# Attention's first two groups stored unsplit through GpSimd's queue, and split later

## The chip, the cores and the metric

The kernel runs on one NeuronCore of a Trainium2 chip. Its engines work side by side, each through its own queue of instructions in order: TensorE (PE in the profile; its weight loads are PEld), VectorE (DVE), ScalarE (ACT), GpSimd (POOL) and SyncE (SP), which here only issues DMAs. Time is device time of one execution in microseconds. The kernel before took 1574.63 us in the median of three runs (1574.16 to 1576.02).

## The reference, cut to what matters

One decoder block in float32, for 1024 tokens of width 1024:

```
h = rms_norm(x);  proj = h @ w_in + b_in     # ret q,k,v,gate | attn q,k,v | gate_a, gate_b
branch_a = (silu(rg) * group_norm(retention(rotary(rq), rotary(rk), rv))) @ w_ret_out
aq, ak = rotary(aq), rotary(ak)              # 16 query heads, 2 key/value heads, 64 wide
ay = softmax_with_sink(band128(aq @ ak^T / 8)) @ av
branch_b = ay.reshape(S, 1024) @ w_attn_out
x = x + (sigmoid(gate_a)*branch_a + sigmoid(gate_b)*branch_b) @ w_out
h2 = rms_norm(x)
x = x + (silu(h2 @ w_ffn_gate) * (h2 @ w_ffn_up)) @ w_ffn_down
out = rms_norm(x)
```

The change concerns `ay`, the outputs of attention, on their way to the product with `w_attn_out`.

## The kernel before, in words

Most products take each operand as two parts: a high half rounded to TensorE's faster float32 format (F32R) and a low half, the rest. ScalarE makes the high half by a cast, VectorE the low half by a subtraction, and three matmuls (high-high, high-low, low-high) give the product. "Split" below means this pair of instructions.

The block runs as one program of stages: norm 1 with the attention keys and values; attention; the retention values; the *column pairs* (retention q and k, the swish gate, two of the merge gates); the retention core, into which the product with `w_attn_out` is filled; the products with `w_ret_out` and `w_out`; the two FFN stages.

**Attention** goes through 32 units: four groups g of four heads, eight blocks b of 128 tokens each. `u_scores` multiplies q and k, VectorE adds the mask and takes the row minimum (line 464), ScalarE takes the exponential (467) and part of the scaling (473). GpSimd copies the sink's column into the score tile beforehand (452), which is all it does here. `u_transpose` turns the probabilities on TensorE and splits them (488, 489). `u_values` multiplies them with the values; TensorE leaves the two parts of a sum in the two halves of the partitions, so ScalarE copies each to the other side into a tile `tm` (502, 503) and VectorE adds (504, 505). Then `tm`, 128 partitions x 2 x 128, is split (507, 508) into the tile that held this group's q, over the part that has been used. The tile `tm` has one buffer: the next unit's line 502 must wait until everything that reads `tm` is done.

After each four blocks SP stores the split result of the group, high and low halves, to `ay_d` in DRAM (541), a DMA of 1 MB. Between the units TensorE is given matmuls of the next group's q (`quad_q`) and of the merge gates (`gate`), a fixed number of steps for each unit. Within the stage a planner orders the instructions of each engine by priority and by its own estimate of times; nothing there is ordered by hand. SP's queue is in order too: a store that waits for VectorE holds up the loads behind it.

**The column pairs** (j = 0 to 9, seven Strassen products P1 to P7 each, 12 matmuls per product) run under `in_order` for VectorE, ScalarE and GpSimd: their instructions keep the order of the text. `wprep_to(i + 3)` splits the weights three products ahead (lines 131 and 134), `wproduct` multiplies (842) and takes the results out, `wlater` finishes the rotary products of q and k (813 to 817), GpSimd forms the sums of the weights (556). During j = 2 the call `load_ay(0)` issues the load of groups 0 and 1 from `ay_d` into the tile AY[0], two DMAs of 2 MB (867); near the end `load_ay(1)` does so for groups 2 and 3. AY has high halves in its even and low halves in its odd planes, and is the moving operand of the product with `w_attn_out` (lines 158 to 160, `acc_bb`).

Of the kernel before, what the change touches and what calls it, by code (L numbers as in the profile page):

```python
# [14 lines left out]
ALU = mybir.AluOpType  # L15
# [19 lines left out]
def f32(t):  # L35
    return t.bitcast(F32)
# [3 lines left out]
def hybrid_block(ctx: ExitStack, tc: tile.TileContext, x, ln1_g, w_in, b_in, ret_norm_g, w_ret_out,  # L40
                 attn_sinks, w_attn_out, w_out, ln2_g, w_gate, w_up, w_down, lnf_g,
                 c_ident, c_atab, c_rtab, c_amask, c_rmask, c_rcol, out):
    nc = tc.nc
    x = x[0]
    out = out[0]
# [16 lines left out]
    ay_d = dram.tile([4, P, 4, S], F32, name="ay_d")  # L62
# [6 lines left out]
    def ps(tag, bufs, name):  # L69
        return psum.tile([P, 512], F32, tag=tag, bufs=bufs, name=name)  # L70
# [32 lines left out]
    @contextmanager  # L103
    def in_order(*engines):

        traced = nc.cur_bb.bb.instructions
        last = traced[-1]
        yield
        start = next(k for k in reversed(range(len(traced))) if traced[k] is last) + 1
        prev = {}  # L110
        for i in traced[start:]:
            if i.engine in engines:
                if i.engine in prev:
                    tc.add_manual_dep(i, prev[i.engine],
                                      mybir.DependencyInfo(mybir.DependencyClass.NoSync, mybir.DependencyReason.DATA),
                                      reason="in_order")
                prev[i.engine] = i.name
# [5 lines left out]
    def hl_tiles(shape, name, pool=None, tag="w"):  # L123
        pool = pool or ring
        return (pool.tile([P] + shape, F32R, tag=tag + "h", name=f"{tag}h_{name}"),
                pool.tile([P] + shape, F32R, tag=tag + "l", name=f"{tag}l_{name}"))
# [121 lines left out]
    for t in range(NB):  # L248
        if t > 1:
            nc.sync.dma_start(xs[:, t, :], x[t * P:(t + 1) * P, :])  # L250
        if 1 <= t <= 2:
            raw = raw_slab([8, P], f"kv{t}")
            c = C_AK if t == 1 else C_AV
# [48 lines left out]
    with tc.tile_pool(name="gt", bufs=1, side="right") as gt, tc.tile_pool(name="w1", bufs=1) as w1:  # L302
# [12 lines left out]
        hi, lo = hl_tiles([8, P], "ak")  # L315
# [121 lines left out]
        def geo(u):  # L437
            g, b = divmod(u, NB)
            nk = 256 if b > 0 else P
            return g, b, nk, B[g // 2], (g % 2) * 4, slice(b * P, b * P + P)  # L440
# [37 lines left out]
        def u_transpose(u):  # L478
            g, b, nk, Bt, jb, qc = geo(u)
            sc = scs.pop(u)  # L480
            phs[u] = []
            for kb in range(nk // P):
                pt = ps("t", 2, f"pT{g}{b}{kb}")
                for j in range(4):
                    nc.tensor.transpose(pt[:, j * P:(j + 1) * P], sc[:, j, kb * P:kb * P + P], ident)  # L485
                ph = w1.tile([P, 512], F32R, tag="ph", bufs=2, name=f"ph{g}{b}{kb}")
                pl = w1.tile([P, 512], F32R, tag="pl", bufs=2, name=f"pl{g}{b}{kb}")
                nc.scalar.copy(ph, pt)
                nc.vector.tensor_tensor(out=pl, in0=pt, in1=f32(ph), op=ALU.subtract)
                phs[u].append((ph, pl))  # L490

        def u_values(u):
            g, b, nk, Bt, jb, qc = geo(u)
            nkb = nk // P
            pv = ps("pv", 1, f"pv{g}{b}")
            for kb, (ph, pl) in enumerate(phs.pop(u)):
                vb = vst[:, b - nkb + 1 + kb, g // 2, :]
                nc.tensor.matmul(pv, vb, ph, start=(kb == 0), stop=False)
                nc.tensor.matmul(pv, vb, pl, start=False, stop=(kb == nkb - 1))
            pvv = pv.rearrange("p (i z q) -> p i z q", i=2, z=2)  # L500
            tm = w1.tile([P, 2, P], F32, tag="tm", bufs=1, name=f"tm{g}{b}")
            nc.scalar.copy(tm[0:64], pvv[64:128, :, 0, :])
            nc.scalar.copy(tm[64:128], pvv[0:64, :, 1, :])
            nc.vector.tensor_tensor(out=tm[0:64], in0=pvv[0:64, :, 0, :], in1=tm[0:64], op=ALU.add)
            nc.vector.tensor_tensor(out=tm[64:128], in0=pvv[64:128, :, 1, :], in1=tm[64:128], op=ALU.add)
            v = Bt[:, jb:jb + 4, qc].rearrange("p (i z) q -> p i z q", z=2)
            nc.scalar.copy(v[:, :, 0, :], tm)
            nc.vector.tensor_tensor(out=v[:, :, 1, :], in0=tm, in1=f32(v[:, :, 0, :]), op=ALU.subtract)

        def gate(n):  # L510

# [16 lines left out]
        for i in range(NU + 1):  # L528
            if i % NB == 0 and 0 < i < NU:
                fl.until(3 * (i // NB - 1) + 1)  # L530
            if i > 0:
                u_transpose(i - 1)
            if i < NU:
                u_scores(i)
            fl.step((i + 1) * left // (NU + 1) - i * left // (NU + 1))
            if i > 0:
                u_values(i - 1)
                if i % 4 == 0:
                    g, b, _, Bt, jb, _ = geo(i - 1)
                    c = slice((b // 4) * 512, (b // 4) * 512 + 512)  # L540
                    nc.sync.dma_start(ay_d[g, :, :, c], f32(Bt[:, jb:jb + 4, c]))
            if i == 2 * NB + 4:
                wv = act.tile([P, 16, 512], F32, tag="B", name="wv")
                for q in range(4):
                    nc.sync.dma_start(wv[:, 4 * q:4 * q + 4, :],
                                      w_in[(q // 2) * 512:(q // 2) * 512 + 512, C_RV + (q % 2) * 512:
                                           C_RV + (q % 2) * 512 + 512].rearrange("(k p) n -> p k n", p=P))
            if i > 3 * NB and i % 2:

                k = (i - 3 * NB) // 2  # L550
                nc.vector.tensor_tensor(out=wv[:, 4 + k, :], in0=wv[:, 12 + k, :], in1=wv[:, 4 + k, :],
                                        op=ALU.subtract)
# [50 lines left out]
    with tc.tile_pool(name="rvp", bufs=1) as rvp:  # L603
# [96 lines left out]
        with in_order(nc.vector.engine, nc.scalar.engine):  # L700
# [18 lines left out]
            for n in range(28):  # L719
                pr, k = VORDER[n // 4], n % 4  # L720
# [10 lines left out]
    AY = []  # L731
# [5 lines left out]
    def load_mask(h):  # L737
        masks[h] = rt.tile([P, 1, P], F32, tag="rmask", bufs=1, name=f"rmask{h}")
        nc.sync.dma_start(masks[h], c_rmask[h].rearrange("p (o s) -> p o s", o=1))

    def load_v(h, z):

        vvs[h, z] = rt.tile([P, 4, 256], F32, tag=f"vv{z}", name=f"rv{h}{z}")
        nc.sync.dma_start(vvs[h, z], v_d[:, 4 * z:4 * z + 4, h * 256:h * 256 + 256])
# [20 lines left out]
    def wprep_to(n):  # L765
        while wready[0] < min(n, len(wseq)):
            j, pr = wseq[wready[0]]
            r0, r1 = wraw[j]
            b11, b12, b21, b22 = r0[:, :, 0:P], r0[:, :, P:2 * P], r1[:, :, 0:P], r1[:, :, P:2 * P]
            b = {"P1": b11, "P5": b11, "P7": b12, "P2": b21, "P4": b21, "P3": b22}.get(pr)  # L770
            if b is None:
                b = wtms[j]
            o = ring.tile([P, 2, 4, P], F32R, tag=("wh", "wl")[wready[0] % 2], name=f"w{j}{pr}")
            split(b, o[:, 0], o[:, 1])
            wops[j, pr] = o
            wdone.add((j, pr))
            if pr in ("P1", "P2") and {(j, "P1"), (j, "P2")} <= wdone:

                wtms[j] = wp.tile([P, 4, P], F32, tag="tt", bufs=1, name=f"wt2_{j}")
                gsub(b11, b12, b11)  # L780
                gsub(wtms[j], b22, b11)
                gsub(b12, b22, b12)
                gsub(b21, b21, wtms[j])
            if pr == "P3" and j + 2 < NW:
                wload_pair(j + 2)
            wready[0] += 1
# [77 lines left out]
    def load_ay(z):  # L864
        AY.append(act.tile([P, 8, 1024], F32R, tag="B", name=f"ay{z}"))
        for g in range(2):
            nc.sync.dma_start(f32(AY[z][:, 4 * g:4 * g + 4, :]), ay_d[2 * z + g])

    qTs, kTs, kts, rgs = {}, {}, {}, {}

    def load_kq(h, z):

        t = (kTs, qTs)[z][h] = kq.tile([P, S], F32, tag=("kT", "qT")[z], name=f"r{z}{h}")
        nc.sync.dma_start(t, rk_d[4 - 4 * z + h])

    with in_order(nc.vector.engine, nc.scalar.engine, nc.gpsimd.engine):
        for i, (j, pr) in enumerate(wseq):
            wprep_to(i + 3)
            wnow[0] = i
            wproduct(j, pr)  # L880
            while wlater and wlater[0][0] <= i:
                wlater.pop(0)[1]()
            if (j, pr) == (2, "P1"):
                load_ay(0)
            elif (j, pr) == (8, "P5"):
                load_kq(0, 0)
                load_kq(0, 1)
            if (j, pr) == (NW - 2, "P5"):
                load_mask(0)
                load_v(0, 0)  # L890
                load_v(0, 1)
            if (j, pr) == (NW - 1, "P7"):
                load_ay(1)
        assert not wlater
# [228 lines left out]
    with tc.tile_pool(name="w3", bufs=1) as w3:  # L1123
# [5 lines left out]
        for n in (0, 4, 1, 5, 2, 6, 3, 7):  # L1129
            kh, k = n // 4, n % 4  # L1130
# [495 lines left out]
    for i, (j, pr) in enumerate(seq):  # L1626
# [9 lines left out]
        if i == 2:  # L1636
# [21 lines left out]
            for z in range(2):  # L1658
                k = slice(2 * z, 2 * z + 2)
# [236 lines left out]
```

## Time and profile before

| | |
|---|---|
| median of three runs | 1574.63 us (1574.16 to 1576.02) |
| profiled execution, and its span | 1573.7 us, 1571.6 us |
| units of groups 0 and 1 | some 97 to 215 us of the span |
| units of groups 2 and 3 | some 215 to 335 us |
| column pairs | some 432 to 624 us |
| load of AY[0] issued | 423.3 us |
| first matmul on AY | 624.6 us |

The span goes from the first to the last instruction of the profiled execution. In a group of instructions, the columns are line, engine, operation, output <- inputs, shapes and count, then the busy time and the mean of one in ns, then the idle time of the engine just before them and what ended it. A row of the waits has the waiter, the releaser, us in total, times, and the longest. A row of a timeline has the start, the duration, the engine, line and operation. A row of DMA issues has the count, the size of each and the median time from issue to landing, where that is known.

### The profile page before, as it was taken

The page shows a single profiled execution, that of the slowest core. Times are in us where ns is not written, and L with a number is a line of the kernel's source. Part 1 is how long each engine was busy: PE and PEld are TensorE (multiplying, and loading weights), DVE is VectorE, ACT ScalarE, POOL GpSimd, SP SyncE. Part 2 cuts the span into 40 slices and gives each one's busy share as a digit, 9 for nine tenths or more (in the row PEclk, how much of TensorE's full clock was granted, in tenths as well). Part 3 has the DMA queues.
Part 4 walks back from the last instruction along what each step waited for, and adds up shares of the span by engine and source line. Part 5 has one row for each costly group of instructions (what it writes and reads, how often), then busy time and mean ns, then how long its engine had stood idle before and what let it go on. Part 6 is the DMA issues. An engine that isn't in the chain of part 4 may idle for free.

```text
span 1571.6 us, 20870 instructions
## 1 busy us (share of the span) xinstructions
PE 1557.4 (99%) x7435; PEld 1296.3 (82%) x7435; DVE 1018.8 (65%) x1809; ACT 732.3 (47%) x1460; POOL 379.5 (24%) x320
## 2 busy tenths in 40 slices
PE   9999999999999999999999999999999999999998
PEld 8887888888888888888888887888888888888886
DVE  6459978787657663877556789444444444678756
ACT  5358887844233334544224365333333333444445
POOL 2000000000055441000021123655555555100001
PEclk9999999999999999999999999999999999999999
DMA  6554654440365454664555402333333333773333
GB/s 214 163 166 131 199 201 149 141 141 34 118 226 154 141 161 173 227 211 152 174 188 184 178 1 80 115 113 102 101 101 108 105 109 101 281 261 85 97 102 126
DMA packets 152581, 228.36 MB, mean 145 GB/s; under 512 B 9307, under 2 KB 81821, under 8 KB 150942
## 3 DMA queue, kind: packets, MB, share of 16 engines
q1 hardware_dynamic: 152476, 227.04, 44.4%
q8 instruction: 58, 0.95, 0.3%
q14 instruction: 45, 0.37, 0.1%
q10 hardware_dynamic: 2, 0.00, 0.0%
HBM read 152.29 MB, written 69.99 MB: 141 GB/s over the span
## 4 chain that ended last, share of the span: by engine, by line
PE 88%; ACT 6%; DVE 4%; issue 1%; POOL 0%; POOLq 0%; ACTq 0%; DVEq 0%
PE fA L1518 15%; PE fB L1518 7%; PE dA L1820 7%; PE wA L842 7%; PE dxP L1820 6%; PE fC L1518 3%; PE wB L842 3%; PE wo L1352 3%; PE va L687 3%; ACT sc L467 2%; PE acc_g L158 2%; PE acc_g L159 2%; PE woP L1352 2%; PE vP L687 2%; PE acc_g L160 2%; PE acc_ba L160 2%
## 5 line engine op out<-in xcount | busy, mean ns | idle before, releaser
L1820 PE MATMUL dA<-dwP,daP 128*128 128x512 f32 x528 | 120.6, 389 | 0.0
L1820 PEld LDWEIGHTS dA<-dwP,daP 128*128 128x128 f32 x528 | 99.0, 188 | 20.7 <-DVE dwP L134 0.2
L1820 PE MATMUL dxP<-dwP,daP 128*128 128x512 f32 x396 | 90.2, 389 | 0.0
L1820 PEld LDWEIGHTS dxP<-dwP,daP 128*128 128x128 f32 x396 | 74.3, 188 | 15.4
L452 POOL COPY sc<-nsink 128x4 f32<-128x4 f32 x32 | 11.4, 357 | 276.1 <-PE pT L485 152.1
L158 PE MATMUL acc_g<-h,wh_g 128*128 128x512 f32 x192 | 75.4, 393 | 0.1
L159 PE MATMUL acc_g<-h,wh_g 128*128 128x512 f32 x192 | 75.2, 392 | 0.0
L160 PE MATMUL acc_g<-h,wl_g 128*128 128x512 f32 x192 | 75.1, 393 | 0.0
L467 ACT ACTIVATE sc<-sc,nm 128x257 f32<-128x257 f32 (+1 forms) x128 | 62.5, 492 | 27.0 <-DVE nm L464 26.6
L1593 POOL TENSOR_TENSOR xf<-xf 128x512 f32<-128x512 f32 x40 | 64.5, 1611 | 30.3 <-issue 28.8
L1524 POOL TENSOR_TENSOR xf<-xf 128x512 f32<-128x512 f32 x33 | 47.3, 1433 | 60.2 <-ACT xf L1526 28.2
L464 DVE CUSTOM_DVE_ANT_0 sc<-s,amask,nsink 128x256 f32<-128x256 f32 (+1 forms) x128 | 54.1, 460 | 9.8 <-PE s L461 9.5
L134 DVE TENSOR_TENSOR dwP<-wd,dwP 128x512 fp32r<-128x512 f32 x77 | 52.6, 683 | 4.3 <-ACT dwP L131 4.3
L1725 POOL TENSOR_TENSOR rs_f<-tot,mhalf 128x1 f32<-128x1 f32 x8 | 4.9, 607 | 205.4 <-DVE tot L1722 205.4
L131 ACT CAST daP<-daP 128x512 fp32r<-128x512 f32 x42 | 26.0, 621 | 55.4 <-PE dxP L1820 26.7
L131 ACT CAST dwP<-wd 128x512 fp32r<-128x512 f32 x77 | 47.4, 616 | 8.7 <-PE dA L1820 6.3
L158 PE MATMUL acc_bb<-ay,wh_bb 128*128 128x512 f32 x128 | 50.9, 399 | 0.0
L556 POOL TENSOR_TENSOR wr_wp<-wr_wp 128x512 f32<-128x512 f32 x10 | 16.6, 1656 | 140.0 <-DVE w0P L134 122.5
L159 PE MATMUL acc_bb<-ay,wh_bb 128*128 128x512 f32 x128 | 50.3, 393 | 0.0
L158 PE MATMUL aq<-h,wh_aq 128*128 128x512 f32 x128 | 50.2, 392 | 0.0
L160 PE MATMUL aq<-h,wl_aq 128*128 128x512 f32 x128 | 50.2, 392 | 0.0
L159 PE MATMUL aq<-h,wh_aq 128*128 128x512 f32 x128 | 50.2, 392 | 0.0
(826 smaller groups left out, 4372.7 us busy)
## 6 DMA issues: line engine op xcount, KB each, us to landing
act_d<-xf SPq DMA_DIRECT2D x77, 256.0 KB, 2.1
daP<-act_d SPq DMA_DIRECT2D x21, 512.0 KB, 3.9
q_d<-stg SPq DMA_DIRECT2D x8, 1024.0 KB
q<-q_d SPq DMA_DIRECT2D x32, 256.0 KB, 5.9
ay_d<-q SPq DMA_DIRECT2D x8, 1024.0 KB
ay<-ay_d SPq DMA_DIRECT2D x4, 2048.0 KB, 13.7
wr_daP<-act_d SPq DMA_DIRECT2D x14, 512.0 KB, 6.6
wr_g<-in_w_in SPq DMA_DIRECT2D x12, 512.0 KB, 6.0
```

The lines of the kernel that those rows point to most:

```text
L131: nc.scalar.copy(hi, raw)
L158: nc.tensor.matmul(pt, hi[:, k, :], xh, start=(k == 0), stop=False)
L159: nc.tensor.matmul(pt, hi[:, k, :], xl, start=False, stop=False)
L160: nc.tensor.matmul(pt, lo[:, k, :], xh, start=False, stop=(k == 7))
L464: nc.vector.tensor_tensor_reduce(out=sc[:, j, 0:nk], in0=pt[:, jj * 256:jj * 256 + nk], in1=mk, scale=1.0, scalar=nsink[:, 4 * g + j:4 * g ...
L467: nc.scalar.activation(sc[:, j, 0:nk + 1], sc[:, j, 0:nk + 1], AF.Exp, scale=-1.0, bias=nm[:, j:j + 1], accum_out=den[:, j:j + 1])
L687: nc.tensor.matmul(vbanks[pr][tt], x_[:, c], w[:, u, :], start=(fresh and k + z == 0), stop=(k == 3 and z == 2), skip_group_check=not fresh)
L842: nc.tensor.matmul(pt, o[:, w, k, :], v, start=(first and k + z == 0), stop=(k == 3 and z == 2), skip_group_check=not first)
L1352: nc.tensor.matmul(bank, v[:, q + u, k, c], w[y][:, k % 2, :], start=(first and z == 0), stop=(last and z == 2), skip_group_check=not tracked)
L1518: nc.tensor.matmul(pt, o[:, w, k, :], v, start=(first and n == 0), stop=(n == 11), skip_group_check=not first)
L1593: nc.gpsimd.tensor_tensor(out=o, in0=a, in1=b, op=op)
L1820: nc.tensor.matmul(banks[tt], a[:, u, c], w[:, v, :], start=(fresh and f + z == 0), stop=(f == NP - 1 and z == 2), skip_group_check=not fresh)
```

## The change

For groups 0 and 1, `u_values` no longer splits. It issues a DMA from GpSimd's queue that writes `tm` as it is, 128 KB in rows of 512 bytes, into the odd planes of `ay_d`. The four stores of 1 MB from SP for these groups go. `load_ay(0)` loads only the odd planes, in four DMAs of 512 KB, and a new function `split_ay`, called after product P3 of the column pairs j = 4, 5, 6 and 7, makes the high half of one plane pair by a cast of 128x1024 on ScalarE and the low half in place by a subtraction on VectorE. Groups 2 and 3 are as before.

```
@@ u_values
             v = Bt[:, jb:jb + 4, qc].rearrange("p (i z) q -> p i z q", z=2)
-            nc.scalar.copy(v[:, :, 0, :], tm)
-            nc.vector.tensor_tensor(out=v[:, :, 1, :], in0=tm, in1=f32(v[:, :, 0, :]), op=ALU.subtract)
+            if g < 2:
+                nc.gpsimd.dma_start(ay_d[g].rearrange("p (i z) s -> p i z s", z=2)[:, :, 1, qc], tm)
+            else:
+                nc.scalar.copy(v[:, :, 0, :], tm)
+                nc.vector.tensor_tensor(out=v[:, :, 1, :], in0=tm, in1=f32(v[:, :, 0, :]), op=ALU.subtract)
@@ the loop over units
-                    nc.sync.dma_start(ay_d[g, :, :, c], f32(Bt[:, jb:jb + 4, c]))
+                    if g > 1:
+                        nc.sync.dma_start(ay_d[g, :, :, c], f32(Bt[:, jb:jb + 4, c]))
@@ load_ay
         for g in range(2):
-            nc.sync.dma_start(f32(AY[z][:, 4 * g:4 * g + 4, :]), ay_d[2 * z + g])
+            if z:
+                nc.sync.dma_start(f32(AY[z][:, 4 * g:4 * g + 4, :]), ay_d[2 * z + g])
+                continue
+            for u in (1, 3):
+                nc.sync.dma_start(f32(AY[z][:, 4 * g + u, :]), ay_d[g, :, u])
+
+    def split_ay(k):
+        hi, lo = AY[0][:, 2 * k, :], AY[0][:, 2 * k + 1, :]
+        nc.scalar.copy(hi, f32(lo))
+        nc.vector.tensor_tensor(out=lo, in0=f32(lo), in1=f32(hi), op=ALU.subtract)
@@ the loop over column pairs
             if (j, pr) == (2, "P1"):
                 load_ay(0)
+            elif j in (4, 5, 6, 7) and pr == "P3":
+                split_ay(j - 4)
```

## The prediction

> **What bounds the kernel now.** I read the page first, then a table of stages, then the groups, waits and timelines of the two stages that the change touches. In the page:
>
> ```profile
> span 1571.6 us, 20870 instructions
> PE 1557.4 (99%) x7435; PEld 1296.3 (82%) x7435; DVE 1018.8 (65%) x1809; ACT 732.3 (47%) x1460; POOL 379.5 (24%) x320
> ```
>
> TensorE is busy nearly throughout, so only time in which its stream is stretched can be won. A busy PE hides short pauses, because overlapping matmuls fill them; the weight loads (PEld) show them better. The table of stages gives busy time for the units of attention groups 0 and 1 (97 to 215 us), of groups 2 and 3 (215 to 335), and for the column pairs around the new splits (510 to 580):
>
> ```profile
> core 0: us, PE busy (x) PEld busy (x) DVE busy (x) ACT busy (x) POOL busy (x), PEclk, DMA share, GB/s
> 97.00:215.00 118.00, 116.61 (x626) 94.86 (x625) 106.13 (x321) 101.90 (x291) 5.72 (x17) 1.00 0.55 163
> 215.00:335.00 120.00, 118.05 (x619) 98.46 (x617) 92.02 (x259) 90.08 (x243) 5.32 (x13) 1.00 0.48 158
> ...
> 510.00:580.00 70.00, 70.00 (x311) 57.98 (x310) 47.14 (x53) 25.14 (x45) 31.07 (x23) 1.00 0.47 139
> ```
>
> The column pairs load weights 82.8% of the time (57.98 of 70), groups 2 and 3 82.05%, groups 0 and 1 80.4%. So groups 0 and 1 lose about 118 x (1 - 80.4/82.05) = 2.4 us against the later groups and 3.5 us against the dense stage; this is my estimate of all that the change can win. There VectorE is 89.9% busy and ScalarE 86.4%, against 76.7% and 75.1% later. The waits of PE in that first window are few and short, and each names VectorE:
>
> ```profile
> PE pv L498 <- DVE tm L505: 0.4, 1, 0.4
> PE pT L485 <- DVE sc L475: 0.4, 1, 0.4
> PE s L460 <- DVE nm L464: 0.3, 1, 0.3
> ```
>
> **What goes.** The groups of the same window:
>
> ```profile
> L508 DVE TENSOR_TENSOR q<-tm,q 128x256 fp32r<-128x256 f32 x16 | 6.7, 419 | 0.5 <-ACT q L507 0.3
> L507 ACT CAST q<-tm 128x256 fp32r<-128x256 f32 x16 | 6.4, 402 | 0.7 <-DVE tm L505 0.6
> L489 DVE TENSOR_TENSOR pl<-pT,ph 128x512 fp32r<-128x512 f32 x31 | 20.7, 686 | 0.9 <-ACT ph L488 0.6
> L475 DVE TENSOR_SCALAR sc<-sc,rd 128x256 f32<-128x256 f32 (+1 forms) x36 | 10.7, 338 | 0.2
> L502 ACT COPY tm<-pv 64x256 f32<-64x256 f32 x16 | 5.9, 370 | 1.3 <-PE pv L499 0.9
> L452 POOL COPY sc<-nsink 128x4 f32<-128x4 f32 x17 | 5.7, 336 | 179.0 <-PE pT L485 116.6 <-ACT sc L467 16.0 <-ACT tm L503 14.2
> ```
>
> Sixteen casts (6.4 us of ScalarE) and sixteen subtractions (6.7 us of VectorE) leave. VectorE falls from 89.9% to 99.4/118 = 84.3%, ScalarE from 86.4% to 80.9%: 42% and 49% of the way down to the load of groups 2 and 3. I give PE the same share, 45%, of the 2.4 us: -1.1 us. The bounds are 0, if what is left of the stretch is the latency of the softmax chain and not load, and -3.5 us.
>
> SP's queue loses four of the eight stores of 1 MB and half of two loads:
>
> ```profile
> ay_d<-q SPq DMA_DIRECT2D x8, 1024.0 KB
> ay<-ay_d SPq DMA_DIRECT2D x4, 2048.0 KB, 13.7
> ...
> SPq L541 <- DVE q L508: 17.9, 2, 16.5
> ```
>
> The store held SP while it waited for VectorE, up to 16.5 us, and loads of weights and of q stood behind it. PE's three waits name no DMA, so I take this at 0; a gain would be inside the -3.5 us bound. The tile of q for groups 0 and 1 is no longer written over and comes free for the value weights a little earlier: also 0. The load of AY becomes four issues for two, 2 MB for 4 MB, at about 423 us:
>
> ```profile
> L867 SPq DMA_DIRECT2D ay<-ay_d x4: 319/371/587, 423.3 to 616.9; - x4
> ```
>
> Two more issues of 0.37 us, with 13.7 us to landing and some 90 us until the first split: 0.
>
> **What comes in attention.** Sixteen DMAs of 128 KB go through GpSimd's queue, and no DMA of the trace does so; its price must be bounded. GpSimd's time for one lies between its smallest instruction, 0.34 us (L452), and its rotary product, 1.5 us, below; I take 1.0, between them. The landing lies between that of the stores of 256 KB from SP, 2.1 us, and that of the loads of q in this very stage, 5.9 us; I take 2.6, the middle of the 256 KB store and the 128 KB copy (3.1), as the nearest in size and kind:
>
> ```profile
> act_d<-xf SPq DMA_DIRECT2D x77, 256.0 KB, 2.1
> q<-q_d SPq DMA_DIRECT2D x32, 256.0 KB, 5.9
> xw<-r SPq DMA_DIRECT2D x32, 128.0 KB, 3.1
> ```
>
> So tm is held 3.6 us after its last addition (2.4 to 7.4). That matters because tm has one buffer: the next unit's first copy (L502) is now behind the DMA, in ScalarE's queue, with the exponentials and the casts for TensorE behind it. The spacing of the copies, and the end of the second addition (L505), where it is tightest; the row with the count is from the view of line 502, the others from the timelines of ScalarE and VectorE:
>
> ```profile
> L502 ACT COPY tm<-pv x16: 369/370/371, 103.9 to 207.7; 64x256 f32<-64x256 f32 x16
> ...
> 141.23 0.37 ACT L502 COPY tm<-pv 64x256 f32<-64x256 f32 x1
> 146.25 0.37 ACT L502 COPY tm<-pv 64x256 f32<-64x256 f32 x1
> 149.97 0.37 ACT L502 COPY tm<-pv 64x256 f32<-64x256 f32 x1
> 154.79 0.37 ACT L502 COPY tm<-pv 64x256 f32<-64x256 f32 x1
> ...
> 142.44 0.43 DVE L505 TENSOR_TENSOR tm<-pv,tm 64x256 f32<-64x256 f32 x1
> 147.46 0.43 DVE L505 TENSOR_TENSOR tm<-pv,tm 64x256 f32<-64x256 f32 x1
> 151.27 0.43 DVE L505 TENSOR_TENSOR tm<-pv,tm 64x256 f32<-64x256 f32 x1
> ```
>
> The mean spacing is (207.7 - 103.9)/15 = 6.9 us and the copies and additions take some 1.65 (146.25 to 147.89), so tm has 5.3 us on the mean and 3.4, 2.1 and 3.1 in these three units. At 3.6 us the three wait 0.2 + 1.5 + 0.5 = 2.2 us. ScalarE was idle 16 of 118 us, so it does not all reach TensorE; I charge a quarter, +0.5 us (0, if the order of the work leaves the gaps wider; the upper bound is the second rival).
>
> [...]
>
> GpSimd itself has room: 5.72 us busy in the window, 21.7 with the DMAs. Behind a DMA that waits for tm stands the copy of the sink column (L452) for a later unit, which that unit's exponential needs; the copies run one or more units ahead (179 us of idle time before 17 of them), so I take 0, with 16 x 0.34 = 5.4 us of ScalarE as the cost if none were ahead.
>
> **What comes in the column pairs.** Four casts and four subtractions of 128x1024, priced by the same shapes elsewhere:
>
> ```profile
> L131 ACT CAST wh_g<-wr_g 128x1024 fp32r<-128x1024 f32 x12 | 12.5, 1046 | 12.7 <-DMA wr_g<-in_w_in 5.8 <-PE aq L159 3.4 <-PE acc_g L159 3.4
> L134 DVE TENSOR_TENSOR wl_g<-wr_g,wh_g 128x1024 fp32r<-128x1024 f32 x12 | 14.6, 1218 | 7.0 <-ACT wh_g L131 6.9
> ```
>
> Uncovered they would be 4 x (1.05 + 1.22) = 9.1 us. The cover is that operands are prepared three products ahead. The first split comes after product P3 of j = 4, which starts at 528.31; the timelines of VectorE, ScalarE and PE behind it:
>
> ```profile
> 532.49 1.78 DVE L134 TENSOR_TENSOR w5P<-wr_wp,w5P 128x512 fp32r<-128x512 f32 x1
> 536.18 1.00 DVE L134 TENSOR_TENSOR w5P<-wr_wp,w5P 128x512 fp32r<-128x512 f32 x1 [0.70 <-ACT w5P L131]
> ...
> 534.91 0.72 ACT L825 ACTIVATE r<-r,bcol 128x512 f32<-128x512 f32 x1 [4.69 <-DVE r L822]
> ...
> 528.31 2.88 PE L842 MATMUL wB<-s4h,w4P 128*128 128x512 f32 x12
> 536.47 2.88 PE L842 MATMUL wB<-h,w5P 128*128 128x512 f32 x12
> 539.19 1.07 PE L842 MATMUL wA<-s,w5P 128*128 128x512 f32 x4
> ```
>
> The two low halves end at 534.27 and 537.18, and PE starts their products at 536.47 and 539.19: 2.0 to 2.2 us to spare, against 1.22 us of delay on VectorE, while ScalarE's 1.05 us fits into its idle 4.69. So 0, with 0.8 us of cover left behind a split. Lengthened by 1.1 us beside GpSimd's work, as line 817 below shows it, a split would outgrow the cover by 0.3 us, 1.2 us for four.
>
> **The sum.** -1.1 + 0.5 = -0.6 us against the profiled execution's 1573.7 us (span 1571.6 and 2.1 around it): 1573.1. The median of the runs shown, 1574.63, lies 0.9 above that execution, so the forecast for the median is 1574.0, no measurable difference (within 0.2%, 3.1 us, about what a measurement of this kernel can tell). The likeliest case's own range is 1572 to 1577.
>
> **The rivals.** *Faster.* The stretch of groups 0 and 1 is all load, tm comes free in time, and SP's freed queue brings its loads early: the whole 3.5 us, 1571.1. For it: all three waits of PE name VectorE. Against: groups 2 and 3, with VectorE far less busy, still lose 1 us. Chance 0.27.
>
> *Slower, by tm.* The DMA holds tm 7 us, as long as the loads of q (5.9) and an issue take. The three tight units wait 3.6 + 4.9 + 3.9 = 12.4 us, the other twelve, with (15 x 5.3 - 8.6)/12 = 5.9 us on the mean, at least 1.1 each: 25.6, less 6.4 of casts saved, 19 us on a ScalarE that had 16 idle. At a third, +6.4: 1581.0. It decides from a hold of some 4.6 us, where the three waits (5.2) and those of others begin to eat the casts saved. For it: one buffer, and DMA engines 55% busy. Against: stores landed in 2.1. Chance 0.15.
>
> *Slower, by blocking.* GpSimd at work holds VectorE up. The view of tile xw shows it:
>
> ```profile
> L813 POOL TENSOR_TENSOR xw<-xw,rtabqT x16: 1286/1482/1827, 448.9 to 574.6; 128x512 f32<-128x512 f32 x16
> L817 DVE TENSOR_TENSOR r<-r,xw x16: 673/679/1786, 451.1 to 577.8; 128x512 f32<-128x512 f32 x16
> ```
>
> The same addition takes 0.68 or up to 1.79 us. If each DMA's preparation blocked VectorE for that 1.1 us, 17.6 us would come for 6.7 saved; 10.9 on the 11.9 it had idle, at a third +3.6: 1578.2. [...] Chance 0.09.
>
> *The splits surface*, against the margins above: up to 9.1 us, 1583. Chance 0.03.
>
> **How the numbers follow.** No difference 0.46, faster 0.27, slower 0.15 + 0.09 + 0.03 = 0.27. The range 1569.0 to 1580.5 holds the likeliest case, the faster one with room for a further gain in the order of the work, the blocking, and the milder half of the tm rival; it leaves out the splits and a hold of 7 us and more.
>
> **What would show it.** Lines 507 and 508 x16 instead of x32; in the window of groups 0 and 1, PEld near 81% or more, VectorE near 84%. A wait of L502 for a DMA, and its length, tells whether the hold is 2.4, 3.6 or 7. VectorE's L475 and L489 longer than 338 and 686 ns beside the DMAs would show blocking. In the column pairs the weight loads should stay at 82.8%; waits of PE for DVE there would be the splits. I am wrong if the time leaves 1571.5 to 1577.8, or if attention shortens by over 3.5 us.

## The result, and the profile after

The changed kernel takes 1590.73 us in the median against 1574.63: 1.0098 times the time before, 95% interval 1.0087 to 1.0109, 16.1 us slower. (The ratio is taken over all runs of both kernels; 0.0098 of 1574.6 is 15.4 us, as much as the spans of the two profiled executions differ.) The forecast was no measurable difference, 1574.0. The profiled execution took 1589.04 us, its span is 1587.0.

The page of the changed kernel, its busy times and the row of GpSimd's queue:

```profile
span 1587.0 us, 20880 instructions
...
PE 1562.9 (98%) x7435; PEld 1301.7 (82%) x7435; DVE 1021.2 (64%) x1797; ACT 730.7 (46%) x1448; POOL 387.2 (24%) x336
...
q0 software_dynamic: 768, 2.10, 0.4%
```

VectorE and ScalarE execute twelve instructions less each, TensorE the same number; only GpSimd has more, the sixteen DMAs. What grew is the time between the instructions, and TensorE's busy time, by 5.5 us for the same matmuls. The table of stages shows where; the columns are those of the tables in the prediction:

```profile
core 0: us, PE busy (x) PEld busy (x) DVE busy (x) ACT busy (x) POOL busy (x), PEclk, DMA share, GB/s
97.00:215.00 118.00, 106.41 (x543) 87.38 (x542) 91.24 (x274) 86.51 (x245) 14.43 (x29) 0.94 0.48 140
215.00:335.00 120.00, 118.23 (x633) 99.22 (x632) 92.54 (x274) 92.36 (x255) 7.16 (x17) 1.00 0.46 148
```

In the units of groups 0 and 1 the weight loads fill 87.38 of 118 us, where they filled 94.86, and TensorE's granted clock is 0.94 on the mean instead of 1.00. Shifted by some 15 us, all later stages are as before. The prediction had asked for "a wait of L502 for a DMA, and its length". The waits of 90 to 250 us (waiter, releaser, us in total, times, longest):

```profile
POOL ay_d L508 <- DVE tm L505: 50.9, 15, 9.2
...
ACT tm L502 <- DMA ay_d<-tm: 16.1, 6, 6.7
...
PE pT L485 <- ACT sc L473: 6.3, 3, 3.5
...
PE s L460 <- DVE nm L464: 5.2, 2, 4.9
```

The wait is there, six times, up to 6.7 us. The view of the tile `tm` has the DMAs (line 508 of the changed kernel) and the time from issue to landing:

```profile
L508 POOL DMA_DIRECT2D ay_d<-tm x16: 680/681/872, 108.5 to 226.1; - x16
...
DMA to landing us min/median/max: 2.2/2.3/7.9
```

GpSimd needs 0.68 us for one, and the median lands 2.3 us after the start of its issue, both less than the forecast took (1.0 and 2.6). But the longest takes 7.9 us, and by the records of the single DMAs six of the sixteen took 4.9 us or more. Three of the six (5.5, 7.9 and 6.4 us) stood beside SP's loads of q, and the waits for them are 13.1 of the 16.1 us; the other three (4.9 to 5.9 us) stood beside loads of the value weights. The timeline around the longest (start, duration, engine, line; idle time before it and its releaser in brackets):

```profile
132.69 1.42 SPq L433 DMA_DIRECT2D q<-q_d  x3
...
133.50 0.70 POOL L508 DMA_DIRECT2D ay_d<-tm  x1 [7.61 <-DVE tm L505]
...
134.61 0.20 ACT L467 ACTIVATION_READ_ACCUMULATOR sc<-sc,nm 128x1 f32 x1
141.52 0.37 ACT L502 COPY tm<-pv 64x256 f32<-64x256 f32 x1 [6.70 <-DMA ay_d<-tm]
...
142.29 0.51 ACT L467 ACTIVATE sc<-sc,nm 128x257 f32<-128x257 f32 x1
142.29 0.42 DVE L504 TENSOR_TENSOR tm<-pv,tm 64x256 f32<-64x256 f32 x1 [5.74 <-ACT tm L503]
...
144.20 0.39 PE L460 MATMUL s<-kst,q 128*128 128x256 f32 x1 [4.94 <-DVE nm L464]
```

SP has just issued the loads of q, 1 MB in four DMAs; the small DMA of `tm` is issued among them and lands at 141.4 (133.5 + 7.9). ScalarE does nothing from 134.8 to 141.5, with the next exponentials (line 467) queued behind the copy; VectorE's addition (line 504) waits for the copies, with the next row minima (464) queued behind it; and TensorE, which waits for these minima, stands for 4.94 us. A table in slices of 5 us shows what follows such a stop:

```profile
135.00:140.00 5.00, 4.26 (x21) 3.21 (x19) 1.56 (x6) 0.00 (x0) 0.00 (x0) 1.00 1.00 239
140.00:145.00 5.00, 0.80 (x3) 0.47 (x4) 2.66 (x12) 3.45 (x11) 0.68 (x1) 0.95 0.49 138
145.00:150.00 5.00, 5.00 (x24) 4.59 (x24) 2.94 (x13) 3.94 (x13) 0.19 (x1) 0.71 0.04 12
...
190.00:195.00 5.00, 1.54 (x9) 1.37 (x8) 1.34 (x4) 2.77 (x9) 0.70 (x1) 0.73 0.75 167
195.00:200.00 5.00, 5.00 (x16) 3.95 (x15) 2.08 (x5) 3.26 (x9) 0.19 (x1) 0.59 0.23 79
```

After the stop at 139 to 144 us TensorE runs the next 5 us at a granted clock of 0.71, after the one at 190 at 0.59: by these shares an estimate of 1.5 and 2.1 us more, lost while it is "busy". A stop of only 2.2 us, before 116 us, also has a lower clock behind it: 0.72 from 115 to 120 us. Taken closer, the granted clock is 0.50 from 117.2 to 120.6, from 144.5 to 147.9 and from 192.3 to 199.1 us, and 1.00 in the rest of these units.

### The profile page after: what moved, and what is told of

The parts are those of the page before. It is cut to its first block, busy times and chain, and to the rows that moved or that the text cites. A ratio compares the mean times of both kernels' runs of the same rounds, so it can differ in the third digit from the quotient of the medians.

```text
span 1587.0 us, 20880 instructions
## 1 busy us (share of the span) xinstructions
PE 1562.9 (98%) x7435; PEld 1301.7 (82%) x7435; DVE 1021.2 (64%) x1797; ACT 730.7 (46%) x1448; POOL 387.2 (24%) x336
## 4 chain that ended last, share of the span: by engine, by line
PE 86%; DVE 6%; ACT 4%; issue 2%; DMA 2%; POOL 0%; POOLq 0%; ACTq 0%; DVEq 0%
PE fA L1533 14%; PE fB L1533 7%; PE dA L1835 7%; PE wA L846 7%; PE dxP L1835 6%; PE fC L1533 3%; PE wB L846 3%; PE va L691 3%; PE wo L1367 2%; PE woP L1367 2%; PE vP L691 2%; PE acc_ba L158 2%; PE acc_ba L160 2%; PE acc_ba L159 2%; PE acc_g L158 2%; PE acc_g L160 2%
## 5 line engine op out<-in xcount | busy, mean ns | idle before, releaser
L1835 PE MATMUL dA<-dwP,daP 128*128 128x512 f32 x528 | 120.6, 389 | 0.0
L1835 PEld LDWEIGHTS dxP<-dwP,daP 128*128 128x128 f32 x396 | 74.3, 188 | 15.4
L158 PE MATMUL acc_g<-h,wh_g 128*128 128x512 f32 x192 | 76.1, 396 | 0.0
L452 POOL COPY sc<-nsink 128x4 f32<-128x4 f32 x32 | 10.9, 342 | 229.3 <-PE pT L485 157.8
L158 PE MATMUL acc_bb<-ay,wh_bb 128*128 128x512 f32 x128 | 51.0, 400 | 0.0
L158 PE MATMUL aq<-h,wh_aq 128*128 128x512 f32 x128 | 50.2, 392 | 0.0
L160 PE MATMUL acc_bb<-ay,wl_bb 128*128 128x512 f32 x128 | 50.1, 391 | 0.0
## 6 DMA issues: line engine op xcount, KB each, us to landing
wd<-in_w_ffn_down SPq DMA_DIRECT2D x6, 1024.0 KB, 11.8
```

What stands on the lines that cost most here:

```text
L158: nc.tensor.matmul(pt, hi[:, k, :], xh, start=(k == 0), stop=False)
L160: nc.tensor.matmul(pt, lo[:, k, :], xh, start=False, stop=(k == 7))
L1835: nc.tensor.matmul(banks[tt], a[:, u, c], w[:, v, :], start=(fresh and f + z == 0), stop=(f == NP - 1 and z == 2), skip_group_check=not fresh)
```

## The experiments

### The hold by itself, and the hold taken away

The kernel before with only the DMAs added; casts, subtractions and stores stay.

```
+    ax_d = dram.tile([2, P, 2, S], F32, name="ax_d")
@@ u_values, behind the cast and the subtraction
+            if g < 2:
+                nc.gpsimd.dma_start(ax_d[g][:, :, qc], tm)
```

> The kernel before, with its split and its stores as they were, and beside them the sixteen DMAs of tm through GpSimd's queue, into a place that nobody reads. Theory of the hold (tm has one buffer, a DMA of it lands late when SP's loads fill the DMA engines, ScalarE stands at line 502 and TensorE runs dry): 1585 to 1596 us, at least 12 us of waits of line 502 for the DMA. Rival, the planner's new order of attention without the split: no more than 1574 to 1579 us here, since the work to be ordered is the old one. Rival, the splits in the column pairs: 1574 to 1576, since there are none. Rival, GpSimd's preparation of a DMA blocks VectorE: slower too, but with longer instructions of VectorE and not with waits of line 502.

1581.71 us, ratio 1.0038 (1.0025 to 1.005): slower, though less than the theory had (1585 or more), and with far less of the wait (it had at least 12 us). The wait of this kernel, whose first copy is line 503:

```profile
ACT tm L503 <- DMA ax_d<-tm: 2.5, 1, 2.5
```

Landings are up to 6.5 us here too, but only one copy comes while a DMA still reads `tm`; whether the casts and subtractions keep the copies further off, or the planner's order, was not measured. Behind that wait TensorE stands for 2.8 us and then runs for 3.4 us at a granted clock of 0.50, together some 4.5 of the 6.0 us (0.0038 of 1574.6).

Next the buffers. More buffers for `tm` need room, so the tanh tile of the merge gates (`st`) gets one buffer in place of two; a control has the same buffers and no change.

```
-            tm = w1.tile([P, 2, P], F32, tag="tm", bufs=1, ...)
+            tm = w1.tile([P, 2, P], F32, tag="tm", bufs=3, ...)
-                t = gt.tile([P, 512], F32, tag="st", bufs=2, ...)
+                t = gt.tile([P, 512], F32, tag="st", bufs=1, ...)
```

> The changed kernel with three buffers of tm; the 2 KB come from the gates' output tile st, which has one buffer for two. Theory of the hold: 1570 to 1577 us, no wait of line 502 for a DMA, while single DMAs still take 5 to 8 us to land. Rivals of order, of the splits and of blocking: 1585 us or more, since all three are still there.

> The control: the kernel before with the same buffers as the run above, three of tm and one of st. All theories: 1573 to 1578 us; what it differs from 1574.6 is the price of the buffers alone, and the run above is to be read against this one.

Changed kernel 1579.26, kernel before with the same buffers 1579.34; both have the ratio 1.0026. Both lie above what was expected (1570 to 1577, and 1573 to 1578). (The 4 to 5 us above the kernel before are the price of the single buffer of `st` or of the order that comes with it; which of the two was not measured.) With three buffers nothing is left of the loss, and nothing of the forecast gain is to be seen. The landings are as late as ever (tile `tm`, changed kernel with three buffers), only nobody waits for them:

```profile
L508 POOL DMA_DIRECT2D ay_d<-tm x16: 680/680/872, 108.2 to 209.7; - x16
...
DMA to landing us min/median/max: 2.2/3.2/7.8
```

The hold put back at the same memory, `tm` with one buffer and `st` with one:

> The changed kernel with one buffer of tm, as it was, and one of st: the run with three buffers of tm with the hold put back, at equal memory for the gates. Theory of the hold: 1585 to 1597 us, 6 to 18 us over the run with three buffers (1579.3), with waits of line 502 for the DMA again, and stretches in which TensorE idles for 2 us and more followed by a lower granted clock. Rival, the order of the work alone: no more than 1582, as with three buffers.

1589.97 us, 10.7 above three buffers, with these waits:

```profile
ACT tm L502 <- DMA ay_d<-tm: 9.5, 4, 6.3
```

And two buffers of `tm`, `st` with one:

> The changed kernel with two buffers of tm, room being made by one buffer instead of two for the tanh tile of the merge gates, as in the pair with three buffers (1579.3 us with and without the change). The late landings of up to 8 us are to stay, but a unit must now come two units (some 13.8 us) after the one whose store it waits for. Theory (the hold of the only buffer is the loss): no wait of line 502 for a DMA, or one of under 1 us, and 1578 to 1581. If the loss is instead contention of the stores with other traffic, or GpSimd at work beside VectorE, a second buffer changes little: 1586 to 1590.

1580.34 us, ratio 1.0032 (1.002 to 1.0044), no wait of line 502 for a DMA. So it is the hold of the only buffer, and not the DMAs' traffic or GpSimd's work beside VectorE: those are all there with two and three buffers. The planner's order differs between these kernels too; the comparison in one order comes at the end.

### The splits by themselves

The kernel before with the four calls of `split_ay` added. They act on planes that are split already, so AY[0] loses the high halves of its values.

```
+            elif j in (4, 5, 6, 7) and pr == "P3":
+                split_ay(j - 4)
```

> The kernel before, with the four splits of 128x1024 added in the column pairs and nothing else. What it computes is not the whole: AY[0] loses its high halves, since the split is made of the low ones. Theory of the hold, and the forecast's 0 for the splits: 1574 to 1576 us, weight loads in 510 to 580 us at 82.8% as before. Rival, the splits surface: 1578 us or more, with waits of PE for DVE in the column pairs.

1574.29 us, ratio 0.9996 (0.9986 to 1.0005). The column pairs around the splits:

```profile
510.00:580.00 70.00, 70.00 (x311) 57.98 (x310) 48.64 (x56) 28.31 (x48) 31.17 (x22) 1.00 0.47 141
```

The same 57.98 us of weight loads as before, with more work on VectorE and ScalarE: the splits cost nothing.

### Why some DMAs land late

If SP's loads of q are what the small DMA stands behind, lighter loads must take the tail away. Both kernels load 64 of the 512 columns of a quarter of q; to fill the rest, the tiles of q get rotated keys at the start.

```
+                    for m in range(8):
+                        nc.sync.dma_start(f32(B[n][...]), k_d[m % 2])
-                    nc.sync.dma_start(f32(Bt[r * 32:r * 32 + 32, jb:jb + 4, c]), qd[:, r, :]...)
+                    nc.sync.dma_start(f32(Bt[r * 32:r * 32 + 32, jb:jb + 4, half * 512:half * 512 + 64]),
+                                      qd[:, r, 0:64]...)
```

> A control: the kernel before, with the loads of q after its rotation cut to an eighth of their bytes (64 of 512 columns; the tiles of q are filled once, early, from the keys' buffer, so most of q is wrong and the work of every engine stays). All theories: 1572 to 1579 us; it prices the cut for the run beside it.

> The changed kernel with the same cut of the loads of q (most of q is wrong, as in the control). Theory that the DMAs of tm land late because SP's loads of q are in the DMA engines ahead of them: landings of 2.2 to 3.5 us but where weights are loaded, waits of line 502 under 5 us in all, and no more than 1576 to 1584 us, 10 us or more of the loss gone. Rival, GpSimd's queue lands late by itself: landings of 5 to 8 us as before and 1586 or more.

The control took 1589.93 us, not 1572 to 1579: the fill of the tiles, 8 MB, held up the first weights of q ("PE aq L158 <- ACT wh_aq L406: 15.8, 1, 15.8" among its waits, at 64 to 80 us). That is ahead of the units, so the pair can still be compared: the changed kernel took 1592.61 (outside the expected 1576 to 1584, as its control is), 2.7 us more than its control instead of 16.1. The runs of the two scatter over 3.5 and 5.0 us, so the 2.7 is rough. The units of groups 0 and 1 in the changed kernel with light loads, from its table of stages:

```profile
97.00:215.00 118.00, 116.25 (x619) 97.28 (x618) 92.17 (x263) 87.38 (x238) 14.27 (x29) 1.00 0.30 100
```

and from its waits (the first copy is line 506 there):

```profile
ACT tm L506 <- DMA ay_d<-tm: 4.5, 3, 2.2
```

With a DMA share of 0.30 in place of 0.48 most of the loss is gone. Landings of up to 6.5 us remain, at a median of 2.3. Is it GpSimd's own queue, or the load of the DMA engines, whose share was 1.00 from 135 to 140 us, while the longest landing of the changed kernel was under way? The same DMAs from ScalarE's queue:

```
-                nc.gpsimd.dma_start(ay_d[g]..., tm)
+                nc.scalar.dma_start(ay_d[g]..., tm)
```

> The changed kernel with the sixteen DMAs of tm issued from ScalarE's queue instead of GpSimd's. Theory that the DMA engines are shared: some landings of 5 to 8 us here too, and 1580 to 1597 us, since tm is held as long (and ScalarE waits for VectorE's additions besides). Rival, GpSimd's queue lands late by itself: all landings under 3.5 us and 1574 to 1580 us.

1584.7 us, ratio 1.0062 (1.0047 to 1.0077), and the wait is the same kind:

```profile
ACT tm L502 <- DMA ay_d<-tm: 12.0, 4, 4.5
```

So the late landing is not peculiar to GpSimd's queue. (This kernel is some 5.7 us faster than the changed one; whether by the queue or by the planner's order was not measured.) The run agrees with the theory that the two queues share the DMA engines, with a landing of 5.4 us; it does not show the sharing itself.

### The removal by itself

With three buffers the removal of 32 instructions had brought nothing. Alone:

```
+            if g > 1:
                 nc.scalar.copy(v[:, :, 0, :], tm)
                 nc.vector.tensor_tensor(out=v[:, :, 1, :], ...)
```

> The kernel before without the sixteen casts (line 507) and sixteen subtractions (line 508) of groups 0 and 1, and nothing else changed; SP still stores the tile, which then holds rotated q instead of the outputs of attention for these groups. Memory, buffers and DMAs are those of the kernel before. The prediction put this part at -1.1 us (bounds 0 and -3.5). If the load of ScalarE and VectorE sets the stretch of that stage: 1571.0 to 1573.5. If, as the pair of kernels with three buffers of tm suggested, the stretch is latency of the softmax chain: 1574 to 1575.5, weight loads in 97 to 215 us as before (94.9 of 118), although ScalarE and VectorE are busy some 6.5 us less each.

1580.22 us, ratio 1.0029 (1.0017 to 1.0041): taking work away made the kernel 4.6 us slower, against both expectations. The table of stages puts it into one stretch; first the kernel before, then this one:

```profile
115.00:135.00 20.00, 20.00 (x105) 16.23 (x104) 18.95 (x53) 16.01 (x45) 0.67 (x2) 1.00 0.36 121
```

```profile
115.00:135.00 20.00, 15.87 (x78) 11.83 (x77) 16.95 (x44) 15.18 (x40) 0.58 (x3) 0.91 0.47 132
```

The timeline of VectorE and ScalarE there, in the kernel before, where TensorE does not stop:

```profile
117.88 0.68 DVE L420 TENSOR_TENSOR stg<-q,atab 128x512 f32<-128x512 f32 x1
...
119.51 0.61 ACT L402 CAST wh_aq<-wr_aq 128x512 fp32r<-128x512 f32 x1
...
120.29 0.68 DVE L424 TENSOR_TENSOR stg<-q,atab 128x512 f32<-128x512 f32 x1
...
121.76 0.40 DVE L504 TENSOR_TENSOR tm<-pv,tm 64x256 f32<-64x256 f32 x1
```

and without the 32 instructions, with TensorE:

```profile
120.85 0.42 DVE L504 TENSOR_TENSOR tm<-pv,tm 64x256 f32<-64x256 f32 x1 [1.09 <-ACT tm L503]
...
122.94 0.68 DVE L420 TENSOR_TENSOR stg<-q,atab 128x512 f32<-128x512 f32 x1
...
124.39 1.14 ACT L402 CAST wh_aq<-wr_aq 128x512 fp32r<-128x512 f32 x2
...
125.06 0.50 PE L158 MATMUL aq<-h,wh_aq 128*128 128x512 f32 x1 [1.48 <-ACT wh_aq L402]
...
125.35 0.69 DVE L424 TENSOR_TENSOR stg<-q,atab 128x512 f32<-128x512 f32 x1
...
125.95 0.48 DVE L464 CUSTOM_DVE_ANT_0 sc<-s,amask,nsink 128x256 f32<-128x256 f32 x1
...
129.51 0.48 PE L460 MATMUL s<-kst,q 128*128 128x256 f32 x1 [1.28 <-DVE nm L464]
```

The planner has written another order. The rotary work of the next q (420 to 429) now stands behind the additions of the unit and ahead of the next row minima (464), and the high halves of the next weights (402) are cast at 124.4 instead of 119.5. TensorE has neither scores nor dense work ready. In slices of 5 us:

```profile
120.00:125.00 5.00, 3.58 (x21) 2.46 (x19) 4.11 (x8) 3.89 (x10) 0.19 (x1) 1.00 0.00 0
125.00:130.00 5.00, 2.88 (x12) 2.07 (x13) 4.99 (x15) 3.71 (x12) 0.00 (x0) 0.97 0.04 18
130.00:135.00 5.00, 4.57 (x21) 3.60 (x21) 4.21 (x12) 2.82 (x9) 0.19 (x1) 0.69 0.99 313
```

It is busy for 3.58 and 2.88 of 5 us, and then its clock is at 0.69.

Is that the accident of one order, or does the removal always do this? The number of dense steps put ahead of the first unit, 20, is changed to 18 and to 22 in three kernels: before, without the 32 instructions, and changed.

```
-        fl.step(20)
-        left = 32 * 8 - 8 - 20
+        fl.step(18)
+        left = 32 * 8 - 8 - 18
```

> The kernel before with 18 instead of 20 steps of dense matmuls put ahead of the first unit of attention, the two steps being spread over the units instead. The work is the same to the instruction; only the planner's order is another one. If the order by itself moves this stage by several us: 1572 to 1582, away from 1574.6 by 2 us or more. If the order matters little: 1573.5 to 1576.

> The same 18 steps, without the sixteen casts and sixteen subtractions (SP stores rotated q for groups 0 and 1 in place of the outputs of attention). If the 4.6 us that the removal alone cost were the new order that the planner wrote: the difference to the kernel before with 18 steps is another number, between -4 and +4. If the removal is slower by a mechanism of its own, such as the softmax chain of one unit meeting the rotary work of the next q: +3 to +6 again.

> The changed kernel with 18 steps. Theory (hold of the only buffer with a tail in the landing): 6 to 15 us above the kernel of the same 18 steps without the casts and subtractions, and waits of line 502 for a DMA of 5 to 20 us in total. If the 16 us of the changed kernel were the luck of one order: within 4 us of it.

> The kernel before with 22 instead of 20 steps of dense matmuls ahead of the first unit of attention: the same work in a third order. If the order by itself moves this stage by several us: 1572 to 1582, away from 1574.6 by 2 us or more. If the order matters little: 1573.5 to 1576.

> The same 22 steps, without the sixteen casts and sixteen subtractions of groups 0 and 1 (SP stores rotated q for these groups). If the order decides: the difference to the kernel before with 22 steps lies between -4 and +4 and is unlike the 4.6 us with 20 steps. If the removal has a mechanism of its own: +3 to +6.

> The changed kernel with 22 steps. Hold theory: 6 to 15 us above the kernel of the same 22 steps without the casts and subtractions, with waits of line 502 for a DMA of 5 to 20 us in total. If the 16 us of the changed kernel were the luck of one order: within 4 us of it.

Medians in us, and in brackets the ratio to the kernel before as it was (20 steps), measured beside each:

| steps | before | without the 32 instructions | changed |
|---|---|---|---|
| 18 | 1571.72 (0.9982) | 1579.97 (1.0036) | 1585.93 (1.0072) |
| 20 | 1574.63 (1) | 1580.22 (1.0029) | 1590.73 (1.0098) |
| 22 | 1573.60 (0.9994) | 1580.08 (1.0035) | 1581.68 (1.0040) |

The intervals are 0.001 to 0.0015 to either side. By the ratios the removal costs 8.5, 4.6 and 6.5 us (1.0036 - 0.9982 = 0.0054 of 1574.6, and so on): no accident of one order, and with 18 and 22 steps more than either expectation had. In all three the weight loads of 115 to 135 us are 11.8 to 12.1 of 20. Why the planner leaves that stretch empty stays open, and it does not always do so: with two and three buffers of `tm`, where the 32 instructions are gone too, the weight loads there are 15.81 and 15.45 us, and with three the change cost nothing. The changed kernel, on top of the removal, costs 5.7, 10.9 and 0.8 us, where the theory of the hold expected 6 to 15: with 18 steps it just falls short, with 22 it fails. But these differences are not the hold alone, since the changed kernel's stretch is fuller in each case (15.4, 15.8 and 14.4 us of weight loads). With 22 steps its waits are fewer:

```profile
ACT tm L502 <- DMA ay_d<-tm: 6.8, 4, 2.9
```

### The order held fast

What is left is to take the 32 instructions away and keep the order. The planned order of all instructions of the stage was taken from the kernel before and given to the new kernel as order-only dependencies, for each engine and for SP's queue. (What these dependencies cost the kernel before, in its own order, was not measured.)

```
+        for e in ["PE", "DVE", "Activation", "Pool", "SP"]:
+            seq = [key[k] for k in map(int, STAGE_ORDER[e].split()) if k in key]
+            for a, b in zip(seq, seq[1:]):
+                tc.add_manual_dep(b, a.name, ...NoSync..., reason="in_order")
```

> The kernel without the sixteen casts and subtractions of groups 0 and 1, in which every engine and SP's queue keep, for all instructions of the attention stage, the order that the planner wrote for the kernel before (SP stores rotated q for these groups). If the 4 to 8 us that the removal cost in three free orders lie in the new order alone: at the level of the kernel before or under it, 1571 to 1575, and the weight loads of 115 to 135 us back at 16.2 of 20 instead of 12. If they lie in the removal itself: 1578 to 1582, with TensorE dry in 120 to 131 us as without the pinned order.

1570.77 us, ratio 0.9977 (0.9968 to 0.9986). The same removal is now 3.6 us faster. The stages of this kernel:

```profile
115.00:135.00 20.00, 20.00 (x110) 17.05 (x109) 19.03 (x51) 16.08 (x45) 0.87 (x3) 1.00 0.60 175
...
97.00:215.00 118.00, 117.21 (x641) 97.97 (x640) 101.47 (x306) 98.22 (x277) 6.84 (x17) 1.00 0.60 181
```

The weight loads fill 97.97 of 118 us, 83.0%, as dense as the column pairs (82.8%). They gain 3.1 us on the 94.86 before, which at that density is 3.8 us of time and accounts for the median.

> The changed kernel in the order of the kernel before: every engine and SP's queue keep it for the attention stage; the sixteen DMAs of tm stand in GpSimd's queue where the planner puts them, and the four stores of 1 MB are gone. What is left against the kernel without casts and subtractions in the same order is the hold of tm, together with the stores and splits, which cost nothing by themselves. Hold theory: 3 to 12 us above that kernel, 1575 to 1586, with waits of line 502 for a DMA. If the hold cost only through the orders that the planner wrote around it: within 2 us of that kernel.

The changed kernel in the old order: 1582.85 us, ratio 1.0049 (1.0036 to 1.0063). Against the removal in the same order this is 0.0072, 11.3 us, for the hold with the stores and splits. Its waits of the first copy (line 512 here) for the DMA:

```profile
ACT tm L512 <- DMA ay_d<-tm: 11.1, 4, 5.4
```

and the timeline shows the longest:

```profile
185.95 0.90 SPq L443 DMA_DIRECT2D q<-q_d  x2
...
186.70 0.69 POOL L520 DMA_DIRECT2D ay_d<-tm  x1 [5.22 <-DVE tm L515]
...
194.97 0.37 ACT L512 COPY tm<-pv 64x256 f32<-64x256 f32 x1 [5.42 <-DMA ay_d<-tm]
195.24 0.91 ACT L483 ACTIVATE sc<-sc,rd 128x256 f32<-128x256 f32 x2
...
195.80 1.54 PE L495 MATMUL pT<-ident,sc 128*128 128x128 f32 x6 [4.49 <-ACT sc L483]
```

(Lines stand ten or more lower in this kernel: 512 is the first copy, 520 the DMA, 483 the scaling, 495 the transposes.) Again the DMA is issued among SP's loads of q, lands 8.2 us after its issue, and the scaling that TensorE waits for is queued behind the copy. Of 5.42 us that ScalarE waits, TensorE loses 4.49.

In ratios, then, the 15.4 us of the changed kernel (0.0098 of 1574.6) are -3.6 for the load taken off, +11.3 for the hold in the old order, and +7.7 that the planner's own order of the changed kernel adds. That order is a third one: its 115 to 135 us are not as empty as without the 32 instructions (15.76 us of weight loads against 11.83), but it meets six waits for DMAs, 16.1 us, where the old order meets four, 11.1 us.

What this costs TensorE can be read from 97 to 235 us: its idle time (138 us less its busy time), and, where the granted clock is 0.50, half of its busy time, as an estimate of what the lower clock costs. (In the changed kernel the matmuls of the gates, 512 columns each, start every 0.43 us at 195.5 to 198.9 us, where the clock is 0.50, and every 0.23 us at 202.2 to 204.3 us, where it is 1.00.)

| kernel, us | idle | lower clock | both |
|---|---|---|---|
| before | 2.05 | 0 | 2.05 |
| changed | 11.64 | 6.20 | 17.84 |
| without the 32 instructions, old order | 0.89 | 0 | 0.89 |
| changed, old order | 10.76 | 1.62 | 12.38 |

In the old order the hold adds 11.5 us by this count, beside 11.3 by the ratios; the whole change adds 15.8, beside 15.4. So by this count the loss is TensorE's stops and the lower clock behind them. The planner's own order adds 5.5 of its 7.7 us here, and 4.6 of them are clock: with nearly the same idle time, TensorE ran at 0.50 for 13.7 us instead of 3.4. The other 2 us were not found. Three buffers in the old order were not tried.

## Why the prediction was wrong, by its steps

**The hold** ("I take 2.6", "so tm is held 3.6 us", "I charge a quarter, +0.5") is the step that failed, and with it the sign. What the forecast gave one value, between 2.4 and 7.4, has two: the median DMA has landed 2.3 us after the start of its issue, under the lower bound, and the late ones 5 to 8 us after it, up to and past the upper one. (A landing of 2.3 us from the start includes the issue, which the forecast had added once more.) The waits of tight units that the forecast did charge came to 0.5 and 1.1 us. The row for the loads of q (5.9 us to landing), which the forecast quoted and used as the outer end, was the answer for the DMAs beside these loads (5.5, 7.9 and 6.4 us). The share that reaches TensorE was not a quarter but most of the wait: 4.49 of 5.42 and 4.94 of 6.70 in the longest, and 9.6 us more idle time against 16.1 us of waits in all. What the copy holds up in ScalarE's queue, and behind the additions in VectorE's, is what TensorE needs next, and a lower clock, 0.50 for 13.7 us in all, comes on top. Bounds and mechanism of the *slower, by tm* rival were near: its 1581.0 for a hold of 7 us in the old order stands against 1582.85. But it reckoned 25.6 us of waits on all units at a third, and the runs show 11.1 us in four waits that cost 11.3 net; that the two times are so close is luck. In the old order the median landing is 3.9 us.

**What goes** (-1.1, a 45% share of 2.4 us) was right in sign and too small: -3.6 us in the old order, at the bound of 3.5 that the forecast had for it. The stretch of groups 0 and 1 was load on VectorE and ScalarE, and taking 6.5 us off each brought it all the way to the density of the column pairs.

**The step that was missing** is the order. The planner was known, but the forecast let "the order of the work" only lengthen the gaps of `tm` or widen the range towards a gain. An edit inside the planned stage rewrites it: the removal alone then costs 4.6 to 8.5 us in three free orders, with 20 steps 8.2 us more than in the old one (1.0029 against 0.9977), and the whole change 7.7 us more than in the old order.

**Splits 0**: right, the run of them alone shows it (0.9996). **Blocking of VectorE by GpSimd**: no sign. With the DMAs the two instructions take what they took: line 489 took 686 ns in the forecast's row; its 338 ns for line 475 is a mean over two shapes, and the median there, in the third row, from the kernel before (ns min/median/max), is 348:

```profile
L489 DVE TENSOR_TENSOR pl<-pT,ph 128x512 fp32r<-128x512 f32 x28 | 18.3, 685 | 2.2 <-ACT ph L488 1.9
L475 DVE TENSOR_SCALAR sc<-sc,rd 128x256 f32<-128x256 f32 x28 | 8.6, 348 | 0.1
...
L475 DVE TENSOR_SCALAR sc<-sc,rd x36: 278/348/354, 100.1 to 213.8; 128x256 f32<-128x256 f32 x30, 128x128 f32<-128x128 f32 x6
```

No cost of such a blocking is to be seen here, at one DMA per unit, since these rows are as before and GpSimd's issues take some 0.68 us, but for one of 0.87. **The sink's copy** (line 452) behind a waiting DMA at 0: GpSimd stood 50.9 us for `tm`, and no wait of ScalarE in this kernel names GpSimd. **SP's queue and the loads** at 0: not measured by themselves; with three buffers, where they differ and the hold does not count, the two kernels are equal.

Of the signs that the forecast named, four came out against it: the time left 1571.5 to 1577.8, the weight loads of groups 0 and 1 fell to 74.0% (87.38 of 118) where 81% or more was asked, VectorE stood at 77.3% (91.24 of 118) instead of 84%, and line 502 waited for a DMA, not for 2.4, 3.6 or 7 us but for a mixture.

## What to carry to other kernels

Here a DMA that read the only buffer of a tile made the tile's next writer wait for the late landings (7.9 us, with a wait of 6.7), not for the median (2.3): price it by the largest transfers that run beside it, and see what else stands in the waiting engine's queue; a second buffer made the wait vanish. Where a planner writes the order, the cost of an edit is its work plus a new order; holding the old order fast separates the two, and here turned a removal from 0.3% slower into 0.2% faster. The mean load of the DMA engines in these units (0.55 before, 0.48 after) said little about the moments when they were full (1.00 from 135 to 140 us in both kernels).

## What the runs showed of the hardware that was not expected

- A DMA of 128 KB from GpSimd's queue costs GpSimd 0.68 us and lands after 2.2 us when the DMA engines are nearly free (share 0.08, at 150 to 160 us), and after up to 7.9 us when it is issued among 1 MB of loads from SP's queue. From ScalarE's queue, where the profile has only two of the sixteen landings, they are 2.2 and 5.4 us.
- TensorE's granted clock fell to 0.59 and 0.71 in the 5 us behind waits of 3.5 and 4.9 us, to 0.72 in the 5 us in which one of 2.2 us ends, and also (0.69) without one long stop: in the kernel without the 32 instructions no wait there was over 1.5 us, but TensorE was busy only 58 and 72% of the two slices before.
- The kernel before got 0.18% faster (0.9982, interval 0.9972 to 0.9992) with 18 instead of 20 steps of dense work ahead of the first unit, the same instructions in another order.
